# Router products from the merged activations' place, in high and low parts, and another order of the last scatters

## The chip, the cores and the metric

The kernel runs on one core of one Trainium2 chip. The metric is the device time of one execution in microseconds. TensorE (PE) multiplies, VectorE (DVE) and ScalarE (ACT) work element by element, GpSimd (POOL) also issues indirect DMAs, and SyncE (SP) issues the direct ones.

## The reference

One layer of a decoder over 2048 tokens of 1024 channels: two parallel branches (a recurrence and latent attention), a gated merge and an output projection, and then a mixture of 32 experts with two experts for each token. The part that the change touches is the router and what it feeds:

```python
x = x + merged @ w_out                       # output projection, residual
h = rmsnorm(x, ffn_norm_g)
p_group = softmax(h @ w_group + b_group)     # 4 groups
fine    = h @ w_router + b_router            # 32 experts; the best group's 8 are kept
top_v, top_i = top_k(fine_sel, 2)
gate = softmax(top_v) * gate_g
# the rows of each expert are gathered, go through SwiGLU, are weighted by gate and added to x
```

## The kernel before, in words

The program has stages: projections, recurrence and attention (to about 1750 us), `phase_f` (merges, output projection, router; to about 2160 us), the experts (to about 2660 us) and a final norm. Large products are made in fp32r from high and low parts: `mm3` issues three matmuls (lines 151 to 153) for each product, and `split` makes the parts, the high one by a copy on ACT (line 143) and the low one by a subtraction on DVE or POOL (line 144).

`phase_f` goes over four quarters of 512 tokens. In a quarter, `merge` makes eight pieces (`d`) of the merged activations: 24 matmuls each into PSUM "fm", two multiplications by the gate `gt` (line 1220), an addition (line 1221) and the split into the tiles `m`, high and low, which have one buffer each. The weights w_b come for each piece by SP into one raw buffer `wbr`, and are split into `wb`. Then, for each of the quarter's four tiles of 128 tokens, `project` makes two halves of 24 matmuls ("fo") and adds x into `xr`, and `router` transposes the tile by eight transposes (line 1240), copies the transposes on ACT into the fp32 tile `h2T` (line 1242, one buffer), and multiplies by the 36 router columns (line 1245, PSUM "fr"): 8 products, 16 records of 128x36 in the profile. A normalised tile `h` (line 1253) is stored to `h2d` for the experts' gathers.

`route` then finds the two experts on DVE (short instructions from line 1327 on, ending in `r_both`), counts the places by two small matmuls on PE (lines 1358 and 1359: `trib`, `onesb`), and computes the slots `si` on DVE (line 1371). Two indirect DMAs on POOL scatter the token's number to the lists `tokl` (one of each pair takes `r_t`, made at line 1373 with two buffers). After each quarter, `gates` makes the weights and scatters them to `wl` by eight more indirect DMAs. All scatters into one list wait for the one before them in that list.

At the end SP loads the lists as `ix`, POOL gathers rows of `h2d` into `xg`, and PE transposes them (line 1540) and starts on the experts. The lists of weights are read as `wx`, behind which SP's queue holds the weights of the expert after next. A list scheduler sets the order of instructions on each engine; engines take them in that order, so an instruction that waits holds all behind it on its engine.

## Time and profile before

| | |
|---|---|
| median of 3 runs | 2710.06 us (2707.57 to 2715.52) |
| the profiled execution | 2706.18 us |
| its span, first to last instruction | 2704.4 us |
| mean granted TensorE clock | 0.963 |
| busy: PE, DVE, ACT, POOL | 92%, 72%, 53%, 36% |

Shares are means over the whole span; the stages differ. The span is 1.8 us shorter than the execution's time, and the profiled execution is 3.9 us below the median.

### The profile page before, as it was taken

The numbers are of one execution on the slowest core, as the hardware profiler recorded it, in microseconds if no ns is written. First come the engines' busy times: TensorE is split into PE (matmuls) and PEld (weight loads), VectorE is DVE, ScalarE is ACT, GpSimd is POOL, SyncE is SP. The second block draws the span as 40 slices with busy tenths as digits, with TensorE's granted clock in tenths as the row PEclk, the third lists the DMA queues.
The fourth block names the chain that finished last, engine by engine and source line by source line (L and its number), as shares of the span: only waits on it lengthen the run. The fifth ranks groups of instructions, "written<-read, shape, count | busy, mean of one in ns | idle before, by whom it ended". The sixth has DMA issues, their size and how long they took to land. (4 is left out here: it accounts for less than half of the span.)

```text
span 2704.4 us, 42459 instructions
## 1 busy us (share of the span) xinstructions
PE 2493.0 (92%) x14868; PEld 2033.2 (75%) x14868; DVE 1957.0 (72%) x3466; ACT 1424.3 (53%) x2539; POOL 961.8 (36%) x676
## 2 busy tenths in 40 slices
PE   8999999999999998989999999999999878999991
PEld 6777778788787886767777777777888667989880
DVE  8766699777748994676666766666666678888883
ACT  6554243465443423666776767632232246878774
POOL 3111612401112222556665665402012145555540
PEclk9999999999999998999999999999999979999995
DMA  4556444435563435444443441674554377999987
GB/s 147 125 146 172 137 140 134 171 102 133 142 177 105 138 122 173 129 122 133 129 123 95 129 129 41 205 225 137 184 167 148 125 228 235 329 288 318 299 246 264
DMA packets 334443, 452.46 MB, mean 167 GB/s; under 512 B 170320, under 2 KB 216272, under 8 KB 332944
## 3 DMA queue, kind: packets, MB, share of 16 engines
q1 hardware_dynamic: 320656, 416.03, 49.3%
q0 software_dynamic: 13568, 33.67, 5.5%
q8 instruction: 118, 1.93, 0.3%
q14 instruction: 101, 0.83, 0.1%
HBM read 318.06 MB, written 138.33 MB: 169 GB/s over the span
## 5 line engine op out<-in xcount | busy, mean ns | idle before, releaser
L151 PE MATMUL am<-h,aw 128*128 128x512 f32 x1104 | 440.8, 400 | 21.2 <-ACT h L237 8.5
L144 POOL TENSOR_TENSOR pl<-pf,ph 128x512 fp32r<-128x512 f32 (+1 forms) x320 | 372.8, 1181 | 238.5 <-ACT ph L143 163.3
L153 PE MATMUL am<-h,aw 128*128 128x512 f32 x1104 | 437.8, 397 | 11.9 <-POOL aw L144 7.5
L152 PE MATMUL am<-h,aw 128*128 128x512 f32 x1104 | 437.3, 396 | 0.1
L1562 PE MATMUL gg<-hh,gu 128*128 128x256 f32 (+5 forms) x1024 | 271.0, 338 | 5.4 <-DVE hh L144 5.0
L151 PEld LDWEIGHTS am<-h,aw 128*128 128x128 f32 x1104 | 210.8, 191 | 70.1 <-ACT h L237 8.5
L153 PEld LDWEIGHTS am<-h,aw 128*128 128x128 f32 x1104 | 210.3, 191 | 60.3 <-POOL aw L144 8.7
L1563 PE MATMUL gg<-hh,gu 128*128 128x128 f32 (+5 forms) x1024 | 249.2, 250 | 0.0
L152 PEld LDWEIGHTS am<-h,aw 128*128 128x128 f32 x1104 | 210.5, 191 | 48.6 <-DVE h L238 2.4
L1052 ACT ACTIVATE pf<-st 128x512 f32<-128x512 f32 (+1 forms) x320 | 167.6, 529 | 119.2 <-PE st L1046 65.2
L1562 PEld LDWEIGHTS gg<-hh,gu 128*128 128x128 f32 x1024 | 195.8, 191 | 13.1 <-DVE hh L144 6.6
L1563 PEld LDWEIGHTS gg<-hh,gu 128*128 128x128 f32 x1024 | 198.6, 194 | 4.5
L143 ACT ACTIVATE ph<-pf 128x512 fp32r<-128x512 f32 (+1 forms) x320 | 176.8, 565 | 6.6
L985 DVE TENSOR_REDUCE mx<-sh 128x1 f32<-128x512 f32 x192 | 128.2, 686 | 66.1 <-PE sh L982 64.9
L144 POOL TENSOR_TENSOR aw<-awr,aw 128x1024 fp32r<-128x1024 f32 (+1 forms) x32 | 89.0, 2782 | 241.2 <-ACT aw L143 231.0
L144 DVE TENSOR_TENSOR gu<-graw,gu 128x1024 fp32r<-128x1024 f32 x128 | 155.0, 1239 | 12.0 <-ACT gu L143 10.3
L143 ACT ACTIVATE gu<-graw 128x1024 fp32r<-128x1024 f32 x128 | 131.1, 1056 | 33.8 <-DMA graw<-in_moe_w_gu 31.4
L801 DVE TENSOR_TENSOR inv<-inv,invt 128x62 f32<-128x62 f32 (+30 forms) x124 | 137.9, 1112 | 2.8
L144 POOL TENSOR_TENSOR sum<-sq,sum 128x512 fp32r<-128x512 f32 x16 | 23.5, 1469 | 317.1 <-ACT sum L143 301.3
L799 DVE TENSOR_TENSOR invt<-inv 128x62 f32<-128x62 f32 (+30 forms) x124 | 133.5, 1076 | 2.6
L1044 PE MATMUL st<-aq,ak 97*128 97x512 f32 (+1 forms) x320 | 127.5, 398 | 8.0 <-ACT pf L1052 7.1
L1580 POOL DMA_INDIRECT x2d<-yo,ix x50 | 93.0, 1860 | 104.2 <-DMA x2d<-yo,ix 21.5
(414 smaller groups left out, 6342.8 us busy)
## 6 DMA issues: line engine op xcount, KB each, us to landing
graw<-in_moe_w_gu SPq DMA_DIRECT2D x128, 512.0 KB
awr<-in_w_cols SPq DMA_DIRECT2D x70, 512.0 KB
draw<-in_moe_w_down SPq DMA_DIRECT2D x62, 512.0 KB
gate<-gsb SPq DMA_DIRECT2D x64, 256.0 KB
SC<-SCd SPq DMA_DIRECT2D x32, 512.0 KB
wbr<-in_w_b SPq DMA_DIRECT2D x32, 512.0 KB
gt<-gate SPq DMA_DIRECT2D x32, 512.0 KB
xs<-in_xT SPq DMA_DIRECT2D x32, 256.0 KB
```

Of the source, the lines that this page charges most:

```text
L143: nc.scalar.activation(hi, src, AF.Copy)
L144: (eng or nc.vector).tensor_tensor(out=lo, in0=src, in1=hi.bitcast(F32), op=OP.subtract)
L151: nc.tensor.matmul(ps, lh, rh, start=first and i == 0, stop=False)
L152: nc.tensor.matmul(ps, lh, rl, start=False, stop=False)
L153: nc.tensor.matmul(ps, ll, rh, start=False, stop=last and i == n - 1)
L799: V.tensor_tensor(out=tv, in0=m[:, 0:t, t:t + 1].to_broadcast([128, t, n]), in1=m[:, t:t + 1, t + 1:].to_broadcast([128, t, n]), op=OP.mult)
L801: V.tensor_tensor(out=m[:, 0:t, t + 1:], in0=m[:, 0:t, t + 1:], in1=tv, op=OP.add)
L985: V.reduce_max(mx[:, j, kb:kb + 1], ps[:, :n], axis=AX)
L1044: T.matmul(ps[:, cs], kk[0][:, ks], qq[0][:, cs], start=True, stop=False)
L1052: A.activation(pf[:, cs], ps[:, cs], AF.Exp, scale=SCALE)
L1562: T.matmul(*a, start=k == 0, stop=False)
L1563: T.matmul(*b, start=False, stop=k == 7)
```

## The change

The router's own fp32 tile `h2T` goes. The transposes are split, high on ACT and low on DVE, into the columns of `m` that belong to the same tile, whose merged activations have been read by then. The router's weights are split once into `wr2` (36 high and 36 low columns). For each of 8 channel blocks there is one product of the high part with all 72 columns and one of the low part with the 36 high ones, both in fp32r. ACT copies the 36 low sums out of PSUM (`lglo`) and DVE adds them. For the last tile, `h` and its store are written behind its routing, and the last quarter's gates are issued behind the last scatter to `tokl`.

```diff
--- before.py
+++ after.py
@@ -1203,6 +1203,9 @@
             wr = p.tile([128, 8, 36], F32, name="wr")
             self.dma(wr, I["w_r"])
             V.tensor_tensor(out=wr, in0=wr, in1=self.pv[:, 55:63, None].to_broadcast([128, 8, 36]), op=OP.mult)
+
+            wr2 = p.tile([128, 8, 72], F32R, name="wr2")
+            self.split(wr2[:, :, :36], wr2[:, :, 36:], wr)
             br = p.tile([128, 36], F32, name="br")
             self.dma(br, bcast(I["b_r"], 36))
 
@@ -1230,29 +1233,41 @@
                               for k in range(8)])
                 V.scalar_tensor_tensor(xt[:, ns], ps, 0.5, xt[:, ns], op0=OP.mult, op1=OP.add)
 
-            def router(i, xt):
+            def router(i, xt, m):
                 st_ = p.tile([128, 4], F32, name="fstat", bufs=2)
                 h = p.tile([128, D], F32, name="h2")
-                hT = p.tile([128, 8, 128], F32, name="h2T")
+
+                hT = [t[:, :, i % 4 * 128:(i % 4 + 1) * 128] for t in m]
                 for b in range(2):
                     ps = self.pst("fo", 3)
                     for k in range(4):
                         T.transpose(ps[:, k * 128:(k + 1) * 128], xt[:, (4 * b + k) * 128:(4 * b + k + 1) * 128],
                                     self.ident)
-                    A.activation(hT[:, 4 * b:4 * b + 4], ps.rearrange("p (k t) -> p k t", k=4), AF.Copy)
+                    self.split(hT[0][:, 4 * b:4 * b + 4], hT[1][:, 4 * b:4 * b + 4], ps.rearrange("p (k t) -> p k t", k=4))
                 ps = self.pst("fr", 2)
                 for k in range(8):
-                    T.matmul(ps[:, :36], hT[:, k], wr[:, k], start=k == 0, stop=k == 7)
+                    T.matmul(ps[:, :72], hT[0][:, k], wr2[:, k], start=k == 0, stop=False)
+                    T.matmul(ps[:, :36], hT[1][:, k], wr2[:, k, :36], start=False, stop=k == 7)
+                lo = p.tile([128, 36], F32, name="lglo", bufs=2)
+                A.activation(lo, ps[:, 36:72], AF.Copy)
                 A.activation(h, xt, AF.Square, accum_out=st_[:, 0:1])
                 A.activation(st_[:, 1:2], st_[:, 0:1], AF.Sqrt, scale=1.0 / D, bias=self.eps[:, 0:1])
                 V.reciprocal(st_[:, 2:3], st_[:, 1:2])
                 yield
                 lg = p.tile([128, 36], F32, name="lg", bufs=2)
-                V.scalar_tensor_tensor(lg, ps[:, :36], st_[:, 2:3], br, op0=OP.mult, op1=OP.add)
+                V.tensor_tensor(out=lo, in0=ps[:, :36], in1=lo, op=OP.add)
+                V.scalar_tensor_tensor(lg, lo, st_[:, 2:3], br, op0=OP.mult, op1=OP.add)
                 self.dma(self.x2d[i * 128:(i + 1) * 128, :], xt)
-                V.scalar_tensor_tensor(h, xt, st_[:, 2:3], g_bc, op0=OP.mult, op1=OP.mult)
-                self.dma(self.h2d[i * 128:(i + 1) * 128, :], h)
+
+                def rows():
+                    V.scalar_tensor_tensor(h, xt, st_[:, 2:3], g_bc, op0=OP.mult, op1=OP.mult)
+                    self.dma(self.h2d[i * 128:(i + 1) * 128, :], h)
+
+                if i < NT - 1:
+                    rows()
                 yield from self.route(p, i, lg)
+                if i == NT - 1:
+                    rows()
                 if i % 4 == 3 and i < NT - 1:
                     self.gates(self.cp, i // 4)
 
@@ -1287,13 +1302,14 @@
                     if last:
                         step(last, 2)
                     project(i, m, xt, 1)
-                    g = router(i, xt)
+                    g = router(i, xt, m)
                     if i == NT - 1:
                         step(g, 1)
                     if last:
                         step(last, 1)
                     last = g
             step(last, 2)
+            self.placed = self.last_place
 
     def gates(self, p, q):
 
@@ -1313,7 +1329,7 @@
                 self.scatter(self.wl[j], self.si[:, j, i:i + 1], self.gate_w[:, j, i:i + 1])
 
     def scatter(self, dst, idx, src):
-        self.nc.gpsimd.indirect_dma_start(out=dst, out_offset=bass.IndirectOffsetOnAxis(ap=idx, axis=0),
+        return self.nc.gpsimd.indirect_dma_start(out=dst, out_offset=bass.IndirectOffsetOnAxis(ap=idx, axis=0),
                                           in_=src, in_offset=None, bounds_check=NE * CAP - 1, oob_is_err=False)
 
     def route(self, p, i, lg):
@@ -1372,7 +1388,7 @@
         t1 = t("t1", 1, I32)
         V.tensor_scalar(t1, self.c["tok"][:, i:i + 1], float(-S), None, op0=OP.add)
         for j, src in enumerate((self.toki[:, i:i + 1], t1)):
-            self.scatter(self.tokl[j], self.si[:, j, i:i + 1], src)
+            self.last_place = self.scatter(self.tokl[j], self.si[:, j, i:i + 1], src)
 
     def route_end(self, p):
 
@@ -1610,7 +1626,8 @@
             xg = {0: x_load(0), 1: x_load(1)}
             V.tensor_copy(ixf, ix)
             self.ranks(p, ixf, ix)
-            self.gates(self.cp, 3)
+            with tc.issue_after(self.placed.ins):
+                self.gates(self.cp, 3)
             for j in range(2):
                 self.dma(wxr[j][:, 0:2], lists(self.wl, j))
```

The rows below show how the engines' orders differ at three places. On PE at the boundary between the first and the second quarter, before: the counting product of tile 2 stands inside the second merge (`wb_18989`), with tile 3's router behind it.

```order
L153 MATMUL fm<-y_18381,wb_18990 128x512
L151 MATMUL fm<-y_18381,wb_18989 128x512 [waits DVE_49]
L1358 LDWEIGHTS trib
L1358 MATMUL fr<-r_both,trib 128x32 [waits DVE_49]
L1359 LDWEIGHTS onesb
L1359 MATMUL fr<-run,onesb 128x32
L1245 MATMUL fr<-wr,h2T 128x36 x4
L1245 MATMUL fr<-wr,h2T 128x36 [waits Activation_49]
L1245 MATMUL fr<-wr,h2T 128x36 x3
L152 MATMUL fm<-y_18382,wb_18989 128x512
```

After: they stand one and a half merges further on, behind the third merge's first half (`wb_19135`), and the second quarter's projection follows at once, reading the new `m_18920` (high) and `m_18921` (low). The router reads the old ones, `m_18034` and `m_18035`; both generations are the same place in memory.

```order
L153 MATMUL fm<-y_18384,wb_19135 128x512
L1374 LDWEIGHTS trib [waits DVE_49]
L1374 MATMUL fr<-r_both,trib 128x32 [waits PE_49]
L1375 LDWEIGHTS onesb
L1375 MATMUL fr<-run,onesb 128x32
L1249 MATMUL fr<-wr_18023,m_18034 128x72
L1250 MATMUL fr<-wr_18023,m_18035 128x36
...
L1250 MATMUL fr<-wr_18023,m_18035 128x36
L151 MATMUL fo<-wo_18016,m_18920 128x512 [waits Activation_49]
...
L153 MATMUL fo<-wo_18016,m_18921 128x512 [waits DVE_49]
```

What moved: the counting product and the last router of a quarter now stand later, and the new `m` is written only when that router has read the old one. On DVE at the same boundary, before: `r_both` of tile 2 stands ahead of the third merge's weights (`wb_19084`).

```order
L1351 TENSOR_TENSOR oh_16823<-r_o_18801,r_o_18823 128x32 [waits DVE_49]
L1220 SCALAR_TENSOR_TENSOR gt<-gt,fm 128x512 [waits PE_49]
L1248 RECIPROCAL fstat<-fstat 128x1 [waits Activation_49]
L1355 TENSOR_TENSOR r_both<-oh_16822,oh_16823 128x32 [waits DVE_49]
L144 TENSOR_TENSOR m_18882<-gt,m_18881 128x512 [waits Activation_49]
L1253 SCALAR_TENSOR_TENSOR h_18923<-xr,fstat,g_bc 128x1024 [waits DMAHW3_49,DVE_49]
...
L144 TENSOR_TENSOR wb_19084<-wbr,wb_19083 128x1024 [waits DMAHW6_49,Activation_49]
...
L1360 TENSOR_TENSOR run<-run,r_both 128x32 [waits PE_49]
```

After, where the weights of the second, third and fourth merge are `wb_19041`, `wb_19135` and `wb_19174` (low parts):

```order
L1367 TENSOR_TENSOR oh_16823<-r_o_18840,r_o_18862 128x32 [waits DVE_49]
L144 TENSOR_TENSOR wb_19174<-wbr,wb_19173 128x1024 [waits DMAHW1_49,PE_49,Activation_49]
L1371 TENSOR_TENSOR r_both<-oh_16822,oh_16823 128x32 [waits DVE_49]
L1376 TENSOR_TENSOR run<-run,r_both 128x32 [waits DVE_49,PE_49]
L1379 SCALAR_TENSOR_TENSOR r_rb<-fr,cst 128x32
...
L1387 TENSOR_TENSOR si<-r_over,r_slot 128x2 [waits DVE_49]
L144 TENSOR_TENSOR m_18921<-gt,m_18920 128x512 [waits PE_49,Activation_49]
```

What moved: `r_both` of tile 2 now stands behind `wb_19174`, the low part of the fourth merge's weights. On POOL at the end of the stage, before (tiles 14 and 15, weights of the last quarter, then the gathers):

```order
L1316 DMA tokl_16810<-toki,si 8192x1 [waits DMASW4_49,DVE_49]
L1316 DMA tokl_16811<-r_t_21714,si 8192x1 [waits DMASW5_49]
L1316 DMA wl_16812<-gate_w,si 8192x1 [waits DMASW0_49,DVE_49]
L1316 DMA wl_16813<-gate_w,si 8192x1 [waits DMASW1_49,DVE_49]
L1316 DMA tokl_16810<-toki,si 8192x1 [waits DMASW6_49,DVE_49]
L1316 DMA tokl_16811<-r_t_21775,si 8192x1 [waits DMASW7_49]
L1316 DMA wl_16812<-gate_w,si 8192x1 [waits DMASW0_49]
L1316 DMA wl_16813<-gate_w,si 8192x1 [waits DMASW1_49]
L1316 DMA wl_16812<-gate_w,si 8192x1 [waits DMASW4_49]
L1316 DMA wl_16813<-gate_w,si 8192x1 [waits DMASW5_49]
L1501 DMA xg_21800<-h2d,ix 128x1024 [waits DMAHW4_49,DMAHW5_49,DMAHW2_49,DMAHW6_49,DMAHW0_49,DMAHW7_49,DVE_49,PE_49]
L1501 DMA xg_21801<-h2d,ix 64x1024 [waits PE_49,Pool_49]
```

After:

```order
L1332 DMA tokl_16810<-toki,si 8192x1 [waits DMASW4_49,DVE_49]
L1332 DMA tokl_16811<-r_t_21908,si 8192x1 [waits DMASW5_49]
L1332 DMA tokl_16810<-toki,si 8192x1 [waits DMASW6_49,DMASW0_49,DVE_49]
L1332 DMA tokl_16811<-r_t_21968,si 8192x1 [waits DMASW7_49,DMASW1_49]
L1332 DMA wl_16812<-gate_w,si 8192x1
L1332 DMA wl_16813<-gate_w,si 8192x1
L1332 DMA wl_16812<-gate_w,si 8192x1 [waits DMASW2_49]
L1332 DMA wl_16813<-gate_w,si 8192x1 [waits DMASW3_49]
L1517 DMA xg_21995<-h2d,ix 128x1024 [waits DMAHW4_49,DMAHW2_49,DMAHW5_49,DMAHW1_49,DMAHW6_49,DMAHW0_49,DMAHW7_49,DVE_49,PE_49]
...
L1332 DMA wl_16812<-gate_w,si 8192x1 [waits DMASW4_49]
L1332 DMA wl_16813<-gate_w,si 8192x1 [waits DMASW5_49]
L144 TENSOR_TENSOR dn_22095<-draw,dn_22094 128x1024 [waits DMAHW4_49,PE_49,Activation_49]
```

What moved: the four scatters to `tokl` stand together, four scatters to `wl` follow them rather than six with two among the `tokl` ones, and the last of `wl` stand behind the gathers and the split of an expert's weights. On DVE the last tile's `h` keeps its place ahead of the last tile's logits in both orders.

## Rows read from the trace of the kernel before

**Rows 1.** TensorE's groups of instructions between 1750 and 2160 us, the stage of merges, output projection and router, with different shapes apart: count, busy us, mean ns, and what ended the idle time before them.

```profile
L152 PE MATMUL fo<-wo,m 128*128 128x512 f32 x255 | 101.7, 400 | 0.0
L1245 PE MATMUL fr<-wr,h2T 128*128 128x36 f32 x256 | 31.7, 275 | 1.6 <-ACT h2T L1242 1.6
```

**Rows 2.** Busy time of each engine in stretches of the same stage (length, then PE, PEld, DVE, ACT, POOL busy, granted clock, DMA share); the first lies within a quarter, the second holds a boundary between two.

```profile
1895.00:1940.00 45.00, 45.00 (x223) 37.16 (x222) 26.50 (x80) 13.56 (x20) 1.94 (x2) 1.00 0.62 200
1940.00:1990.00 50.00, 50.00 (x246) 41.05 (x245) 35.39 (x126) 14.08 (x20) 14.58 (x14) 1.00 0.48 159
```

**Rows 3.** What TensorE waited for between 1750 and 2190 us: us in total, times, longest.

```profile
PE gt L1540 <- DMA xg<-h2d,ix: 18.3, 1, 18.3
PE fr L1358 <- DVE r_both L1355: 5.5, 2, 5.0
PE fm L151 <- DVE gt L1220: 5.0, 2, 4.6
```

**Rows 4.** TensorE's weight loads in the same stage by form: busy us, mean ns.

```profile
L151 PEld LDWEIGHTS fo<-wo,m 128*128 128x128 f32 x253 | 47.7, 189 | 11.4 <-ACT m L143 1.0
L1245 PEld LDWEIGHTS fr<-wr,h2T 128*128 128x128 f32 x256 | 31.1, 191 | 2.7 <-ACT h2T L1242 1.9
L1358 PEld LDWEIGHTS <-trib 128*128 128x128 bf16 x16 | 1.6, 101 | 3.8 <-issue 3.8
```

**Rows 5.** TensorE in time (start, us): first a pair of fp32r products with 256 and 128 columns in the stage of experts, then the end of the projections and the start of the experts.

```profile
2330.43 0.34 PE L1562 MATMUL gg<-hh,gu 128*128 128x256 f32 x1
2330.66 0.33 PE L1562 MATMUL gg<-hh,gu 128*128 128x256 f32 x1
...
2144.70 0.97 PE L1245 MATMUL fr<-wr,h2T 128*128 128x36 f32 x8
2145.51 0.48 PE L151 MATMUL fo<-wo,m 128*128 128x512 f32 x1
...
2148.61 0.40 PE L153 MATMUL fo<-wo,m 128*128 128x512 f32 x1
2148.84 0.98 PE L1245 MATMUL fr<-wr,h2T 128*128 128x36 f32 x8
...
2176.46 1.97 PE L1540 MATMUL gt<-cst,xg 128*128 128x128 f32 x8 [18.30 <-DMA xg<-h2d,ix]
```

**Rows 6.** ACT in time: half of a tile's transposes copied for the router, and the high part of w_b for the fourth merge (d=3) behind the first quarter boundary.

```profile
1851.28 0.60 ACT L1242 ACTIVATE h2T<-fo 128x512 f32<-128x512 f32 x1 [0.28 <-PE fo L1240]
1861.22 1.06 ACT L143 ACTIVATE wb<-wbr 128x1024 fp32r<-128x1024 f32 x1 [5.54 <-DMA wbr<-in_w_b]
```

**Rows 7.** DVE in time over the same boundary: a subtraction for the merged activations, the one for the fourth merge's w_b, and the stop at r_t (the bracket says how long DVE stood and on what).

```profile
1851.10 0.69 DVE L144 TENSOR_TENSOR m<-gt,m 128x512 fp32r<-128x512 f32 x1
1862.32 1.22 DVE L144 TENSOR_TENSOR wb<-wbr,wb 128x1024 fp32r<-128x1024 f32 x1 [0.69 <-issue]
...
1890.78 0.15 DVE L1373 TENSOR_SCALAR r_t<-cst 128x1 int32<-128x1 f32 x1 [5.79 <-DMA tokl<-r_t,si]
```

**Rows 8.** SyncE's queue in time over the same boundary: the load of w_b for the fourth merge.

```profile
1856.45 0.33 SPq L96 DMA_DIRECT2D wbr<-in_w_b  x1
```

**Rows 9.** TensorE in time over the same boundary: the counting product of tile 2, a small stop behind a split of w_b, and the stop behind DVE.

```profile
1854.09 0.19 PE L1358 MATMUL fr<-r_both,trib 128*128 128x32 bf16 x1
...
1877.17 0.50 PE L151 MATMUL fm<-y,wb 128*128 128x512 f32 x1 [0.56 <-ACT wb L143]
...
1892.18 0.80 PE L151 MATMUL fm<-y,wb 128*128 128x512 f32 x1 [4.58 <-DVE gt L1220]
```

**Rows 10.** GpSimd in time over the same boundary: the scatters of the first quarter's weights, and tile 3's places behind them.

```profile
1878.41 1.48 POOL L1316 DMA_INDIRECT wl<-gate_w,si  x1 [3.99 <-DMA wl<-gate_w,si]
1883.40 0.97 POOL L1316 DMA_INDIRECT wl<-gate_w,si  x1 [2.22 <-DMA wl<-gate_w,si]
1886.13 0.97 POOL L1316 DMA_INDIRECT tokl<-r_t,si  x1 [0.30 <-issue]
```

**Rows 11.** DVE in time at the end of the stage: h of tile 15, its logits and its slots.

```profile
2151.81 1.28 DVE L1253 SCALAR_TENSOR_TENSOR h<-xr,fstat,g_bc 128x1024 f32<-128x1024 f32 x1
2153.12 0.25 DVE L1251 SCALAR_TENSOR_TENSOR lg<-fr,fstat,br 128x36 f32<-128x36 f32 x1
...
2159.07 0.22 DVE L1371 TENSOR_TENSOR si<-r_over,r_slot 128x2 int32<-128x2 f32 x1
```

**Rows 12.** GpSimd in time at the end of the stage: the last tile's first scatter to `tokl`, scatters to `wl`, and the first gather.

```profile
2160.38 0.97 POOL L1316 DMA_INDIRECT tokl<-toki,si  x1 [0.31 <-issue]
2162.93 0.97 POOL L1316 DMA_INDIRECT wl<-gate_w,si  x1 [0.31 <-issue]
2164.21 0.97 POOL L1316 DMA_INDIRECT wl<-gate_w,si  x1 [0.30 <-issue]
2165.49 0.97 POOL L1316 DMA_INDIRECT wl<-gate_w,si  x1 [0.31 <-issue]
2169.00 0.97 POOL L1316 DMA_INDIRECT wl<-gate_w,si  x1 [2.54 <-DMA graw<-in_moe_w_gu]
2170.28 1.53 POOL L1501 DMA_INDIRECT xg<-h2d,ix  x1 [0.30 <-issue]
```

**Rows 13.** SyncE's queue at the load of the weights' lists, and ACT's first use of the expert weights wx.

```profile
2180.79 5.01 SPq L96 DMA_DIRECT2D wx<-wl  x8
...
2208.12 1.27 ACT L1589 ACTIVATE yo<-gd,wx 128x512 f32<-128x512 f32 x2
```

## Prediction

> **What bounds the kernel now.** I read the stages first. In the stage of merges and router TensorE is the engine that sets the pace: in a stretch within a quarter it is busy for all of 45.00 us, and in one that holds a quarter boundary for all of 50.00 us, at a granted clock of 1.00, while DVE is busy for 26.50 and 35.39 us [rows 2]. So work added to DVE or ACT there is free until TensorE waits for it, and time of TensorE counts one for one. Then I read what TensorE does wait for: 5.0 us for the gate's product on DVE, nearly all in one stop of 4.58 us at 1892.18, and at the end 5.5 us for `r_both` and 18.3 us for the first gather [rows 3, 9]. Two chains matter, therefore: that of the quarter boundaries, and that of the end, where TensorE stands for 18.30 us until 2176.46 [rows 5].
>
> The stop at 1892.18 is a head-of-line stop. DVE stood 5.79 us at `r_t` until 1890.78, because that needs an earlier scatter to `tokl` to have landed [rows 7]. This one left POOL at 1886.13 only, behind scatters to `wl` before which POOL had stood for 3.99 and 2.22 us, since each waits for its predecessor's landing [rows 10].
>
> **The products.** A tile's router had 16 matmul records, 256 for 16 tiles [rows 1]. Eight of them take 0.81 us from the first to the next instruction (2144.70 to 2145.51), so 0.101 us each and 1.62 us a tile [rows 5]. After, there are 16 fp32r matmuls with 72 and 36 columns, each with a load of 128 columns. Their price is not in the trace; the nearest row is a pair of fp32r products with 256 and 128 columns, 0.23 us for the pair, so at most 0.115 us each and 1.84 us a tile [rows 5]. The load of an fp32r weight takes 189 ns, and of the router's fp32 weight 191 ns [rows 4], so I take no change on TensorE, with bounds of -1 and +3.5 us (16 times 0.22) over the stage.
>
> The trace's bf16 load takes 101 ns, about half of the others [rows 4]. The Trainium skill (TensorE: Matmul & The Clock Gate, "Weight-path perf modes") says that fast weight load is on for 128 weights whose type is not FP32, and that FP32 gains nothing. Read so that fp32r is no FP32, the rule would halve the router's loads; the fp32r row of 189 ns says that it doesn't. By the rule the sum below would be smaller by some 12 us; by the row nothing changes.
>
> **The splits.** The two ACT copies of a tile, 0.60 us each [rows 6], stay, with another destination. New on DVE are two subtractions of 0.69 us (the row of a 128x512 one [rows 7]) and an addition of about 0.2, on ACT a copy of 36 columns of about 0.2: some 1.6 us of DVE a tile, 25 us in all. They lie under TensorE: a quarter has 4 x 1.6 = 6 us more DVE work, against 14 to 18 us idle in each stretch of rows 2. Without that cover they would cost all of it. One split of 128x288 for `wr2` lies at the stage's beginning and is taken at nothing.
>
> **The boundaries.** With the order of after, tile 2's counting product stands behind 11 + 12 = 23 more merge matmuls than before. They take 0.23 us each (2148.61 to 2148.84, a matmul of 512 columns as theirs [rows 5]), so TensorE comes there at 1854.09 [rows 9] + 5.4 = 1859.5. But `r_both` of tile 2 now stands on DVE behind the fourth merge's low weights. These weights are loaded at 1856.45 [rows 8], split on ACT at 1861.22 [rows 6] and subtracted on DVE from 1862.32 to 1863.54 [rows 7]; this chain has one raw buffer and isn't shortened. So `r_both` is ready at about 1863.7, and TensorE waits 4.2 us. Behind it the old `m` is read by tile 3's router, and only then may ACT write the new `m`, which the next projection reads at once: a copy of 0.60 us and the signals on both sides, 0.9 us. Against these 5.1 us stand the 4.58 us of the old stop and 0.56 us behind a split of w_b [rows 9], the same 5.1. The old stop's cause, `tokl` behind `wl` on POOL, is still there; with one and a half merges of shift I leave 1.5 us of it (between 0 and 4.6). The first boundary is thus 5.1 + 1.5 - 5.1 = +1.5 us. At the second and the third boundary TensorE had no or nearly no wait. The new wait on `m` comes there too, and `r_both` stands ahead of its neighbour's low weights rather than behind, so that the stop is milder: I take +2 and +1.5 us, between 0 and 5.1 each. All together +5.0 us, bounds -4 (first boundary -5.1, little at the others) and +14.
>
> **The end.** Tile 14's router (1.62 us) and tile 13's counting now stand behind the last projection, which thus begins at 2148.61 - 1.7 = 2146.9 [rows 5]. From there I walk: x is added by 2148.2; TensorE does tile 14's router and then tile 15's second transposes until 2149.4; ACT has the square of the tile (1.2 us) and the high copy (0.60) until about 2151.1; DVE has `h` of the last tile (1.28 us, still ahead [rows 11]) and then the low subtraction until 2152.4; the second half of tile 15's router ends at 2153.3, and its logits are there at 2153.9, against 2153.12 before [rows 11]. From these logits to the slots DVE took 5.95 us for 40 instructions (2153.12 to 2159.07), 0.149 us each; after there are 54, since tile 14's routing is now interleaved: 8.0 us. So the slots come at 2161.9, 2.8 us late. POOL then gives 1.0 back, for the first scatter of tile 15 left 1.31 us behind the slots [rows 11, 12], being queued behind `wl`, and now leaves some 0.3 behind them: `tokl` and `ix` are 1.8 us late. In front of the gather stand four scatters to `wl`, and the fourth waits for the landing of the second. What such a landing takes differs: at most 2.56 us for the scatter of 2162.93 (its successor left at 2165.49), 4.79 us for that of 2164.21 (2169.00), beside which expert weights were loaded [rows 12]. The loads stand beside them in after as well, so I take 4.8: the gather leaves about 1.5 us later than 2170.28, bounds -3 (the walk on DVE too pessimistic) and +5.
>
> The Trainium skill (DMA: Bandwidth & Descriptors, "Anatomy of one DMA") puts a GpSimd DMA at about 2.0 us plus its bytes' time. By that the fourth scatter would wait for nothing and the gather leave at about the old time, so that the sum would be smaller by 1.5 us. The row with 4.79 us disagrees.
>
> Behind the gathers, the last pair of scatters to `wl` now stands behind the split of an expert's weights, so `wx` is loaded some 6 us after 2180.79, and the weights behind it on SP too. ACT first needs `wx` at 2208.12 [rows 13], which leaves more than 10 us behind the permutation; 0 us, at most +2.
>
> **Sum.** 0 + 0 + 5.0 + 1.5 = +6.5 us on the profiled execution's 2706.18, so 2712.7; that execution is 3.9 us below the runs' median, so 2716.6 as a median. What a measurement can tell from no change is 0.3%, 8 us: 2702 to 2718.
>
> **Rivals.** *Faster:* the head-of-line stop goes (-5.1 at the first boundary), the others are hidden since DVE runs ahead of TensorE, and the end gains: slots no later, and 1.1 us less queueing and a shorter row of `wl`, -3. Then 2710 - 8.1 = 2702, at the edge of what can be told. For it speaks that POOL's order at the end is better; against it that `r_both` stands behind a DMA chain with one buffer. It decides at the point where DVE has `r_both` ready by 1859.5. *Slower:* the same wait at every boundary, 3 x 5.1, the old stop not gone, and the end at +3: 2710 + 18 = 2728. It needs `r_both` to wait for w_b at all three boundaries. *No effect:* the waits cancel and the median stays at 2710; that holds if the interleaved routing at the end costs what POOL gives. *Fast loads* for fp32r, by the rule above: a router matmul at 0.101 x 101/191 = 0.053 us, 0.77 us a tile less, 12 us over all; with the +6.5 of the other terms 2704.5.
>
> **Chances.** My sum 0.40, no effect 0.17, slower 0.25, faster 0.15, fast loads 0.03. My sum's own spread (2710 to 2723) puts about a third of it above 2718, and a tenth of the slower case stays below it. Faster by over 0.3% is 0.18 (the case, and tails of the others), slower 0.36, within 0.46. The range is 2699 to 2731: from just beyond the faster case to just beyond the slower one.
>
> **What the profile will show.** Right: TensorE with a wait for `r_both` of 3 to 5 us once near 1860 and smaller ones near 1965 and 2060, waits for the split of `m` just behind them; the router's 16 records in 1.6 to 1.8 us; tile 15's slots near 2162 plus what the boundaries added; the fourth `wl` scatter behind an idle time. Wrong: no wait at the counting products, or the router's products at another pace than a load each; or a wait for `wx` or weights in the first experts, which I count as hidden.

## The result

The changed kernel takes 2729.94 us (median of 17 runs, 2717.44 to 2738.44); before takes 2707.57 us (17 runs, 2701.22 to 2715.52). By all runs together the ratio is 1.0076, with a 95% interval of 1.0064 to 1.0089: slower by about 21 us. The profiled execution has a span of 2729.5 us at a granted clock of 0.957.

To see in which stage the time went, I take the first and the last start of four groups: the merges on TensorE, the projections, the transposes of gathered rows, and ACT's weighting of the experts' outputs. These are the rows of the changed kernel (durations in ns are minimum, median and maximum; then the first and the last start):

```profile
L151 PE MATMUL fm<-y,wb x256: 387/389/628, 1735.8 to 2119.7; 128*128 128x512 f32 x128
L153 PE MATMUL fo<-wo,m x256: 387/395/796, 1754.1 to 2166.1; 128*128 128x512 f32 x128
L1556 PE MATMUL gt<-cst,xg x400: 270/272/476, 2197.2 to 2638.6; 128*128 128x128 f32 x134
L1605 ACT ACTIVATE yo<-gd,wx x64: 665/682/720, 2235.9 to 2671.3; 128x512 f32<-128x512 f32 x64
```

From the first merge to the last projection are 430.3 us, from there to the first gathered rows 31.1, and on to the last weighting 474.1. The same in all profiled executions but that of e10 (below):

| kernel | ahead of the merges | merges to last projection | to the gathered rows | experts | TensorE's waits in the second stage | clock lost there |
|---|---|---|---|---|---|---|
| before | 1732.0 | 416.6 | 27.9 | 468.9 | 7.1 | 1.6 |
| before, again (e12) | 1732.4 | 419.6 | 28.2 | 475.2 | 9.0 | 3.5 |
| changed | 1735.8 | 430.3 | 31.1 | 474.1 | 13.4 | 8.8 |
| changed, again (e11) | 1730.1 | 431.4 | 31.6 | 474.6 | 17.9 | 5.1 |
| e1 router alone | 1738.9 | 431.0 | 34.1 | 475.1 | 18.0 | 5.1 |
| e2 scatters alone | 1736.2 | 420.4 | 27.5 | 484.8 | 11.1 | 3.5 |
| e3 own half tiles | 1734.7 | 430.2 | 36.4 | 481.3 | 15.3 | 10.4 |
| e4 8 tiles r_t | 1721.9 | 419.6 | 27.8 | 471.1 | 7.4 | 3.6 |
| e5 r_both first | 1736.0 | 442.7 | 33.6 | 464.1 | 22.5 | 15.3 |
| e6 own last tile | 1727.6 | 427.5 | 33.8 | 476.5 | 15.8 | 6.8 |
| e7 16 tiles r_t | 1736.2 | 411.7 | 28.3 | 466.0 | 1.5 | 1.7 |
| e8 e5 with 16 | 1730.2 | 436.7 | 33.7 | 464.3 | 16.0 | 10.6 |
| e9 e2 with 16 | 1741.6 | 407.4 | 27.1 | 488.6 | 1.8 | 1.8 |

All in us. The waits are those that the profile lists for TensorE from 80 us behind the first merge to the last projection; a wait of 2.7 to 3.8 us for `y`, which every one of these executions has at 72 to 75 us, lies ahead of that. "Clock lost" sums 1 minus the granted clock over stretches of 5 us in the same part, so it counts some of the idle time too. The first column is the same program in all kernels and spreads over 20 us in single executions, so a single time says little here, and a stage is compared with its like.

Most of the loss is in view: the second stage has 11.9 us more than in four executions with before's order there (mean 430.9 of the changed kernel, its repeat and e1, against 419.0 of before, its repeat, e2 and e4), the way to the gathered rows 3.4 us more. These make 15 of the 21 us; the experts and what is left to chance come below. TensorE's waits in the changed kernel, in us, times and longest, which answer to [rows 3]:

```profile
PE gt L1556 <- DMA xg<-h2d,ix: 17.6, 1, 17.6
PE fr L1374 <- DVE r_both L1371: 8.3, 4, 3.0
PE fm L151 <- ACT y L143: 7.1, 4, 3.5
PE fm L151 <- DVE gt L1223: 3.3, 2, 1.9
PE fo L151 <- ACT m L143: 2.7, 4, 1.2
```

In before, the view of [rows 3] has this line for `y`:

```profile
PE fm L151 <- ACT y L143: 3.3, 1, 3.3
```

The reader sees that the gate's product has gone from 5.0 to 3.3 us, but the counting products wait in four places rather than two, and waits for the split of `m` (2.7 us) and more for `y` (7.1 us against 3.3) have come. The first boundary in time, on TensorE:

```profile
1865.65 0.19 PE L1374 MATMUL fr<-r_both,trib 128*128 128x32 bf16 x1 [1.54 <-DVE r_both L1371]
1865.71 0.28 PE L1249 MATMUL fr<-wr,m 128*128 128x72 f32 x1
1865.82 0.26 PE L1250 MATMUL fr<-wr,m 128*128 128x36 f32 x1
...
1867.42 0.41 PE L1249 MATMUL fr<-wr,m 128*128 128x72 f32 x1
1867.63 0.38 PE L1250 MATMUL fr<-wr,m 128*128 128x36 f32 x1
...
1868.97 0.80 PE L151 MATMUL fo<-wo,m 128*128 128x512 f32 x1 [0.53 <-ACT m L143]
```

The counting product waits 1.54 us, the router follows, and in its midst the distance of two products grows from 0.11 to 0.21 us. The stretches there (length, busy PE, PEld, DVE, ACT, POOL, granted clock, DMA share, GB/s) show the reason:

```profile
1862.00:1867.00 5.00, 3.46 (x23) 2.77 (x21) 3.10 (x17) 1.06 (x1) 0.00 (x0) 0.97 0.17 43
1867.00:1870.00 3.00, 2.47 (x10) 2.16 (x11) 1.40 (x6) 1.24 (x3) 1.94 (x2) 0.50 0.37 144
1870.00:1873.00 3.00, 3.00 (x9) 2.32 (x8) 1.83 (x10) 0.00 (x0) 0.00 (x0) 0.50 0.64 90
1873.00:1876.00 3.00, 3.00 (x13) 2.17 (x12) 1.33 (x5) 0.00 (x0) 0.00 (x0) 0.92 0.67 260
```

The clock is at 0.50, the lower of its two levels (1.2 GHz), until about 1873. This happens four times in the profiled execution from the first boundary on (near 1866, 1925, 1980 and 2085), in before once, behind the stop of [rows 9]. By the measure of the table the four cost 3.4, 1.7, 1.7 and 1.7 us.

### The profile page after: what moved, and what is told of

Same layout as the page of the kernel before. It is cut to its first block, busy times and chain, and to the rows that moved or that the text cites. A ratio compares the mean times of both kernels' runs of the same rounds, so it can differ in the third digit from the quotient of the medians.

```text
span 2729.5 us, 42521 instructions
## 1 busy us (share of the span) xinstructions
PE 2508.2 (92%) x14868; PEld 2042.9 (75%) x14868; DVE 1978.1 (72%) x3515; ACT 1426.9 (52%) x2556; POOL 966.1 (35%) x676
## 4 chain that ended last, share of the span: by engine, by line
PE 31%; issue 10%; DVE 7%; DMA 7%; ACT 4%; POOL 1%; SPq 0%; POOLq 0%; DVEq 0%; ACTq 0%
PE gg L1578 3%; PE st L1044 2%; PE sh L982 2%; PE pv L1036 2%; PE pv L1031 2%; PE st L1045 2%; PE st L1046 2%; PE pv L1032 2%; DMA graw<-in_moe_w_gu 2%; DVE gu L144 2%; PE gg L1579 1%; ACT dn L143 1%; DMA zx<-x2d 1%; PE gt L1556 1%; DMA tokl<-r_t,si 1%
## 5 line engine op out<-in xcount | busy, mean ns | idle before, releaser
L1578 PEld LDWEIGHTS gg<-hh,gu 128*128 128x128 f32 x1024 | 197.5, 193 | 13.6 <-DVE hh L144 4.9
L985 DVE TENSOR_REDUCE mx<-sh 128x1 f32<-128x512 f32 x192 | 128.3, 686 | 65.3 <-PE sh L982 64.1
```

The source lines that it names most:

```text
L985: V.reduce_max(mx[:, j, kb:kb + 1], ps[:, :n], axis=AX)
L1578: T.matmul(*a, start=k == 0, stop=False)
```

## The experiments

**Each half alone.** e1 is the changed kernel without these two edits, e2 is before with them:

```diff
-                if i < NT - 1:
-                    rows()
+                rows()
                 yield from self.route(p, i, lg)
-                if i == NT - 1:
-                    rows()
...
-            with tc.issue_after(self.placed.ins):
-                self.gates(self.cp, 3)
+            self.gates(self.cp, 3)
```

> The changed kernel with the order of the last scatters and of the last tile's rows as before: the router's part of the change alone. Theory (the router's later place makes the boundary waits, and TensorE's clock falls behind them): the stage of merges loses its 16 us here too, and the time is 1.006 to 1.008 of before; the granted clock falls at the three boundaries. Rival (the scatters' order costs it, through the later lists of weights): within 0.2% of before.

> The kernel before with the order of the last scatters and of the last tile's rows as changed: the other part alone. Theory: the last tile's first place is scattered about 1 us earlier, the fourth scatter of weights waits for a landing as before, and the first gather leaves between 1.5 us earlier and at the same time; the lists of weights come 5 to 7 us later and are hidden; time within 0.1% of before. Rival: the later lists hold back the experts, and the stage of experts is 4 to 5 us longer (1.0015 or more).

The edit to `rows()` doesn't show in the traces: the last tile's `h` starts ahead of that tile's logits with it (the changed kernel at 2169.30 and 2173.97) as without it (e1 at 2173.05 and 2177.72). What e1 and e2 tell apart is the gates' place. Measured: e1 1.0095 (1.0074 to 1.0116), e2 1.0057 (1.0037 to 1.0076). Neither theory held whole: each half costs, and the two together (1.0152) twice what the whole change does. By the table the two are different things. e1 repeats the longer merges (431.0) and lengthens the way to the gathered rows to 34.1 us; in e2 that way is 27.5, against 27.9, 28.2 and 27.8, as was expected, but the experts take 484.8 us. In e1 POOL shows what the scatters' new place is worth once the routing is late:

```profile
2184.55 0.97 POOL L1329 DMA_INDIRECT wl<-gate_w,si  x1 [0.30 <-DVE wx L1530]
2187.10 0.97 POOL L1329 DMA_INDIRECT tokl<-toki,si  x1 [0.30 <-issue]
2196.02 0.97 POOL L1329 DMA_INDIRECT wl<-gate_w,si  x1 [2.85 <-DMA wl<-gate_w,si]
2197.29 1.37 POOL L1514 DMA_INDIRECT xg<-h2d,ix  x1 [0.30 <-issue]
```

The last tile's first place leaves at 2187.10, behind two scatters to `wl` (2184.55 and the next), and the first gather at 2197.29, behind a fourth scatter that stood 2.85 us. With the scatters' new order this way is 31.1 and 31.6 us, without it 34.1, 33.6, 33.8 and 33.7 (e1, e5, e6, e8): 2.5 us won, where the router is changed, and about 0.5 where it is not (e2).

**The experts' order.** The scheduler writes another order of the expert stage for e2: compared row by row, half of TensorE's order there differs from before, while the changed kernel's differs in about one per cent. What TensorE waited for in e2's expert stage, and in the same stage of before:

```profile
PE gd L151 <- ACT at L1579: 11.3, 8, 5.5
PE gd L153 <- DVE at L1582: 7.2, 9, 1.6
```

```profile
PE gd L151 <- ACT at L1571: 4.5, 8, 1.3
PE gd L153 <- DVE at L1574: 4.0, 5, 1.4
```

The second products (`gd`) wait for the activations (`at`) for 18.5 us rather than 8.5. e9 repeats e2's expert order in a program with another merge stage:

> The kernel of e2 (order of the last scatters alone) with the sixteen tiles for r_t of e7; its order of the experts on TensorE is e2's, and half of it differs from the kernel before. Theory (the experts' order that the scheduler writes out behind the scatters' new place costs the 14 us that e2's stage of experts was longer): that stage takes 480 us or more again, the stage of merges 411 to 414 as in e7, and the time is 1.002 to 1.003 of before. Rival (one disturbed execution): 466 to 472 us for the experts and 0.996 to 0.998.

Measured: 1.0014 (1.0000 to 1.0029), a little less than expected, with 407.4 us for the merges (expected 411 to 414) and 488.6 for the experts. The theory on the experts holds: two executions with that order took 484.8 and 488.6 us, nine with before's own (before, e4, e7, e12) or one within about a per cent of it (the changed kernel, e11, e5, e6, e8) 464 to 477. So e2's loss goes with this order and not with the later lists: in the changed kernel the lists are read as late (at 2207.04, 9.9 us behind the start of TensorE's transposes, 10.0 in e2, against 4.3 in before [rows 5, 13]) and its experts take 474. e3's order, 7% from e2's, took 481.3 us. Another order is not always longer: e1's, a third one, differs from before's by nearly half, too, and took 475.1. What in e2's order costs the time stays open, since in e9 the same waits for `at` make 14.8 us, and those for `hh` 18.8 rather than 12.1 in before and 12.5 in e2.

**The tiles of its own.** In e3 each half of a tile has its own place and the products follow it at once; in e6 only the last tile of a quarter has such a place, while the products follow each half in all tiles:

```diff
+                    if i % 4 == 3:
+                        hT = [p.tile([128, 4, 128], F32R, name="h2T%d" % j) for j in range(2)]
+                    else:
+                        hT = [t[:, 4 * b:4 * b + 4, i % 4 * 128:(i % 4 + 1) * 128] for t in m]
```

> The changed kernel, but the high and low parts of the router's input lie in two tiles of their own of half the size (one buffer each, used twice a tile) and not in the merged activations' place. Theory (the new merged activations' wait for the last router and its later place make the stalls, and the stalls the fall of the clock): the waits for the split of m behind a router go, the clock falls at most once, as before, and about 3 us (16 times 0.17 of the products' pace) stay, 1.001 to 1.003 of before. Rival (the narrow fp32r products themselves let the clock fall): the clock falls at each boundary, or oftener, with no wait of over 1 us there, and the time stays at 1.006 or more.

> The router's part of the change alone (last scatters as before), but the last tile of each quarter has its high and low parts in two half-size tiles of their own, so that the new merged activations wait for no router. The order of the experts is that of the kernel before within half a per cent. Theory: the waits of the projections for the split of m at the boundaries go, r_both's stay; the stage takes 424 to 428 us, the time is 1.004 to 1.006 of before. Rival (the wait for the old m decides): the stage takes 420 to 423 us, 1.002 to 1.003.

Measured: e3 1.0093 (1.0072 to 1.0114), e6 1.0058 (1.0036 to 1.0080). In e3 the waits for `m` went, as the theory had it, and those for `r_both` too, but the time went against its number. It does not decide, for other stops came on TensorE in their place,

```profile
1936.64 1.11 PE L1245 MATMUL fo<-cst,xr 128*128 128x128 f32 x4 [5.64 <-DVE xr L1234]
...
2128.40 0.40 PE L1250 MATMUL fr<-wr,h2T 128*128 128x36 f32 x1 [3.30 <-DVE h2T L144]
```

and the clock's falls lie behind these and one of 1.78 us. The second is one of the half tiles' own; the first isn't: `xr` stood on DVE behind `r_t`:

```profile
1935.83 0.15 DVE L1390 TENSOR_SCALAR r_t<-cst 128x1 int32<-128x1 f32 x1 [8.95 <-DMA tokl<-r_t,si]
```

In e6 the waits for `m` did not go. The merge stage took 427.5 us, in the range of the first theory, but for other reasons, one of them to be seen on DVE:

```profile
1908.54 0.15 DVE L1393 TENSOR_SCALAR r_t<-cst 128x1 int32<-128x1 f32 x1 [7.28 <-DMA tokl<-r_t,si]
```

DVE stood 7.28 us at `r_t`, the head-of-line stop of [rows 7], and the low part of `m` for which TensorE waited 5.42 us until 1910.48 stood behind it. Another wait, of 4.16 us until 1900.46, ended ahead of that stop: there the high part of `m` stood on ACT behind a split of w_b, for whose load ACT had stood 9.33 us.

**r_both ahead of the weights.** e5 is e1 with the splits of the third and fourth w_b issued behind `r_both`:

```diff
-        self.split(hl[0], hl[1], raw)
+        with (self.tc.issue_after(after.ins) if after is not None else ExitStack()):
+            self.split(hl[0], hl[1], raw)
```

> The router's part of the change alone (order of the last scatters as before), and the splits of w_b for the third and fourth merge of a quarter are issued behind r_both of the quarter before's third tile. The order of the experts on TensorE is within half a per cent of that of the kernel before, which it was not in the first run of the router's part alone (e1). Theory (stops at the counting product, and the clock's falls behind them, are the larger part of the stage's loss): the waits of 1 to 2 us for r_both at the boundaries go, the clock falls there at most once, the stage of merges takes 421 to 425 us from its first merge to its last projection (417 to 420 before, 430 to 431 with the change), and the time is 1.003 to 1.005 of before. Rival (the boundary's work is late anyway, and w_b now waits for r_both): the stop moves to the next merge, the stage takes 429 us or more, 1.006 or more.

Measured: 1.0108 (1.0083 to 1.0133), with 442.7 us for the merges. The rival held, and worse: the scheduler put the counting products earlier on TensorE, where they wait 5.39, 2.31 and 2.66 us; TensorE waits 8.11 us for the gate's product, too, and DVE's longest stop at `r_t` grew to 9.3 us:

```profile
DVE r_t L1389 <- DMA tokl<-r_t,si: 17.4, 3, 9.3
```

**r_t without reuse.** e4 gives `r_t` eight tiles, e7 sixteen:

```diff
-        t1 = t("t1", 1, I32)
+        t1 = p.tile([128, 1], I32, name="r_t1", bufs=16)
```

> The kernel before with eight buffers rather than two for r_t (its tile is named apart), so that DVE doesn't stop there for the scatter to land. Theory: the stop of 4.58 us of TensorE near 1892 and the fall of its clock behind it (about 1.7 us) go: 5 to 6 us faster, 0.998. Rival: the stop only moves to the next instruction on DVE that needs the scatters, no change.

> The kernel before with sixteen tiles for r_t, one for each tile of tokens, all made at the stage's beginning, so that DVE never waits there for a scatter to land (with eight the ninth was issued at the same early place and waited for the first). The order of the experts is unchanged. Theory: the stop of 3.5 to 4.9 us at the first boundary and the clock's fall behind it go, 0.998 of before. Rival: another wait ends as late, and nothing changes.

e4 measured 1.0000 (0.9986 to 1.0014). All eight were written at the start, those from the ninth on were issued as early as a tile came free, and DVE stopped there as before (3.20 us at 1826.27, 4.76 at 1880.98). e7 measured 0.9969 (0.9955 to 0.9983), faster than before and than the changed kernel. Its merges took 411.7 us, and of TensorE's waits from the first boundary to the experts three groups of [rows 3] and of its neighbours now read:

```profile
PE fr L1358 <- DVE r_both L1355: 5.5, 2, 5.0
PE fr L1245 <- ACT h2T L1242: 1.5, 2, 1.3
PE fm L151 <- DVE gt L1220: 0.2, 1, 0.2
```

The stop cost at least its own 4.6 us: 416.6 and 419.6 us became 411.7, and e2's 420.4 became 407.4 in e9. The clock stays up at that boundary.

> The kernel of e5 with sixteen tiles for r_t. Theory: DVE's stops at r_t held the merges of the second quarter too; 2 to 5 us less than e5, so 1.001 to 1.004 of before. Rival: these stops lay beside TensorE's work there: the same as e5 within 1 us.

e8 measured 1.0051 (1.0032 to 1.0069), 436.7 us for the merges, 6.0 less than e5: DVE's stops held the merges there too, by a little more than expected. By the ratios e8 is some 15 us faster than e5, and the stages show no more than these 6: between the two profiled executions another 5.8 us lie ahead of the merges, where the programs don't differ. Two stretches of e8 also show the clock behind two waits of like length:

```profile
1967.95 0.21 PE L1374 MATMUL fr<-r_both,trib 128*128 128x32 bf16 x1 [2.30 <-DVE r_both L1369]
...
2133.26 0.50 PE L151 MATMUL fo<-wo,m 128*128 128x512 f32 x1 [2.40 <-DVE xr L1235]
```

```profile
1966.00:1971.00 5.00, 3.05 (x16) 3.06 (x17) 4.12 (x25) 0.00 (x0) 0.30 (x1) 0.67 0.18 48
1971.00:1976.00 5.00, 5.00 (x17) 4.09 (x18) 3.57 (x10) 2.29 (x4) 1.65 (x2) 0.65 0.55 119
2131.00:2136.00 5.00, 2.75 (x12) 2.24 (x13) 3.17 (x6) 3.32 (x5) 1.58 (x1) 1.00 0.28 111
2136.00:2141.00 5.00, 5.00 (x32) 4.34 (x31) 0.69 (x1) 1.01 (x2) 0.83 (x1) 1.00 0.52 168
```

At 1967.95 a wait of 2.30 us is followed by the router's products; the clock falls (0.67 and 0.65). At 2133.26 a wait of 2.40 us lies between projections; the clock stays at 1.00. This is no rule. All twelve waits for `r_both` at the boundaries of the changed kernel, e11, e1, e5 and e8 (1.13 to 5.39 us) have a fall behind them. But a wait amid the last quarter's router, which the kernels without the router's change have, was followed by a fall in e4, e7 and e9 and by none in before, e12 and e2:

```profile
2112.94 1.08 PE L1245 MATMUL fr<-wr,h2T 128*128 128x36 f32 x8 [1.33 <-ACT h2T L1242]
```

```profile
2110.69 1.08 PE L1245 MATMUL fr<-wr,h2T 128*128 128x36 f32 x8 [1.26 <-ACT h2T L1242]
```

The first is before's, the second e7's, where the clock from 2111 to 2116 is 0.66.

**The change with r_t mended.**

> The changed kernel with sixteen tiles for r_t. Theory: DVE's stops at r_t hold the merges behind the boundaries here too (waits for the gate's product of 1.4 to 1.9 us and falls of the clock), and go: the stage of merges takes 421 to 427 us instead of 430. Its order of the experts is a third one, which may take anything between 466 and 485 us; the time is 1.003 to 1.009. Rival: the stage of merges is as long as before this, 429 to 431, since r_both and the wait for m decide.

Measured: 1.0072 (1.0043 to 1.0102), as the changed kernel itself. The time lies in the theory's range, but its only profiled execution took 8427.15 us and is not read, so theory and rival, which differ in the stage of merges, are not told apart, and where the 16 tiles' gain went is open; this program's order of the experts is near e1's.

> The changed kernel a second time, for a second profiled execution: what of its stages' lengths repeats. If the program's order sets them: 428 to 432 us for the merges, 31 from the last projection to the first gathered rows, 472 to 476 for the experts. If chance does: the experts between 464 and 472.

> The kernel before a second time, for a second profiled execution. If the order sets the lengths: 416 to 421 us for the merges, 28 to the first gathered rows, 466 to 471 for the experts; what comes ahead of the merges lies between 1722 and 1739 by chance.

The merges (431.4 and 419.6) and the way to the gathered rows (31.6 and 28.2) repeat within 3 us. The experts of before took 475.2 us the second time, above the 466 to 471 expected: there chance is as large as the 4 us by which the changed kernel's mean lies above the mean of before, e4, e7 and e12, and whether these 4 us are the change's stays open.

## Why the prediction was right and wrong

It forecast slower, by 6.5 us, with 2716.6 the likeliest and 2731 the upper end. The measured 2729.94 lies just inside. The direction and the end were right; of the boundaries' term the waits that the prediction named came out near their size, and what it put at nothing, other waits and the clock, made up most of the difference.

**The end** was right. From the start of the last projection the walk had the last tile's logits 7.0 us on, its slots at 15.0, the first gather at 24.9. On TensorE, DVE and POOL:

```profile
2166.12 0.48 PE L153 MATMUL fo<-wo,m 128*128 128x512 f32 x1
```

```profile
2173.97 0.25 DVE L1259 SCALAR_TENSOR_TENSOR lg<-lglo,fstat,br 128x36 f32<-128x36 f32 x1
2180.52 0.16 DVE L1387 TENSOR_TENSOR si<-r_over,r_slot 128x2 int32<-128x2 f32 x1
```

```profile
2181.16 0.97 POOL L1332 DMA_INDIRECT tokl<-toki,si  x1 [0.67 <-DVE wx L1533]
2183.71 0.97 POOL L1332 DMA_INDIRECT wl<-gate_w,si  x1 [0.30 <-issue]
2184.99 0.97 POOL L1332 DMA_INDIRECT wl<-gate_w,si  x1 [0.31 <-issue]
2186.26 0.97 POOL L1332 DMA_INDIRECT wl<-gate_w,si  x1 [0.30 <-issue]
2189.66 0.97 POOL L1332 DMA_INDIRECT wl<-gate_w,si  x1 [2.43 <-DMA wl<-gate_w,si]
2190.94 1.53 POOL L1517 DMA_INDIRECT xg<-h2d,ix  x1 [0.31 <-issue]
```

The logits came 7.85 us behind 2166.12, the slots at 14.4, the gather at 24.8. That the sum fits to 0.1 us is in part luck: the logits were 0.85 us later than in the walk, and the way from them to the slots took 6.55 us rather than 8.0. The first place leaves 0.64 us behind its slots, and the fourth scatter to `wl` waits 2.43 us for a landing. It leaves, at 2189.66, 4.7 us behind the second scatter's 2184.99, as in [rows 12] (4.79), while SyncE's queue holds loads of expert weights from 2185.04 on. The Trainium skill (DMA: Bandwidth & Descriptors, "Anatomy of one DMA") puts such a DMA at about 2.0 us and its bytes' time. The trace does not agree for this scatter, which had only 128 rows of one number to move; the scatter before it, 2.55 us ahead of its own successor, leaves room for the 2.0 us. The term was +1.5, and 3.4 less the 1.7 us of work moved behind the projection is +1.7.

**The products** were priced at nothing, with an upper bound of 3.5 us. In the trace two starts lie 0.111 us apart (1865.71 and 1865.82), 1.78 us a tile against 1.62: +2.5 us over sixteen tiles. No change was taken where the row of 0.115 us for an fp32r product [rows 5] was the nearer. The forms of the products and of their loads read:

```profile
L1249 PE MATMUL fr<-wr,m 128*128 128x72 f32 x128 | 30.7, 285 | 0.0
```

```profile
L1249 PEld LDWEIGHTS fr<-wr,m 128*128 128x128 f32 x128 | 25.4, 198 | 0.6 <-DVE lglo L1258 0.3
```

No fast load shows: such a load takes 198 ns, where the fp32 one took 191 [rows 4], and the products' starts are not at the 0.053 us of that rival. The Trainium skill (TensorE: Matmul & The Clock Gate, "Weight-path perf modes") has fast weight load on for 128 weights whose type is not FP32. Read so that fp32r is no FP32, it does not agree with this trace.

**The boundaries** were the term that was too small: +5.0 forecast, with +14 the upper bound. Worked out from the table, the stage has 11.9 + 1.7 = 13.6 us more work and waiting than before, of which 2.5 are the products: 11 us. The waits grew by 7.8 us (16.4 as a mean of the changed kernel, e11 and e1 against 8.7 of before, e12, e2 and e4), and the clock lost 3.2 us more (6.3 against 3.1 in the same executions; part of it is idle time that the waits hold too). So 2.5, 7.8 and 3.2 make 13.5.

By what TensorE waited for, as means of the same executions in us:

| wait | before | changed | difference | forecast |
|---|---|---|---|---|
| `r_both` and the new `m` | 0 | 7.7 | +7.7 | +8.6 |
| the gate's product, the router's copy, w_b | 8.7 | 4.4 | -4.3 | -3.6 |
| `y` and `xr` | 0 | 4.3 | +4.3 | 0 |
| the clock | 3.1 | 6.3 | +3.2 | 0 |

The forecast's 8.6 is 5.1 at the first boundary, 2 and 1.5 at the others; its -3.6 is what it took off the old stops. So the waits that the prediction named, new and old, came out near their sum, and the steps that failed are two terms that it left at nothing. The first is the waits for `y` and `xr`. The longest of them on DVE and then TensorE:

```profile
1921.45 1.23 DVE L1188 TENSOR_TENSOR yin<-yin 128x1024 f32<-128x1024 f32 x1 [5.84 <-DMA yin<-Rcd]
```

```profile
1923.82 0.50 PE L151 MATMUL fm<-y,wb 128*128 128x512 f32 x1 [2.46 <-ACT y L143]
```

DVE stood 5.84 us for loaded rows just ahead of it, so the splits on DVE, which the prediction counted as hidden, were not what ended this wait. SyncE issued those loads at 1914.31 only; what made them late, the splits, the new order or the stops at `r_t` (28.7 us of DVE in the changed kernel, 25.1 in before), no run here tells apart. The second is the clock: it was left out, and falls at all three boundaries and behind `y`, in before only behind the old stop.

Within the first line the parts differ from the forecast. The wait behind `r_both` at the first boundary was put at 4.2 us and measured 1.54: DVE reads

```profile
1863.38 0.15 DVE L1389 TENSOR_SCALAR r_t<-cst 128x1 int32<-128x1 f32 x1 [1.58 <-DMA tokl<-r_t,si]
1864.28 1.23 DVE L144 TENSOR_TENSOR wb<-wbr,wb 128x1024 fp32r<-128x1024 f32 x1
1865.42 0.17 DVE L1371 TENSOR_TENSOR r_both<-oh,oh 128x32 bf16<-128x32 bf16 x1
```

so the fourth merge's low weights did stand ahead of `r_both`. The changed kernel's first merge starts 3.8 us later than before's, so times are counted from there. The low weights ended at 1865.51, 129.7 us on, 1.8 earlier than the 131.5 of the walk (1863.54); TensorE came at 1864.11, 128.3 us on, 0.8 later than its 127.5 (1859.5). The chain of [rows 6, 7, 8] thus ended a little earlier, where the prediction took it as fixed. The waits for the new `m`, put at 0.9 us each, measured 0.53, 0.62 and 1.17 at the three boundaries, but 2.4 to 2.5 more stands in e11 (at 1901.30) and e1 (at 1909.17) behind the first one. `r_both` made TensorE wait 1.17 us at the second boundary and not at all at the third. Of the signs that the prediction named, the one wait of 3 to 5 us near 1860 failed so; the waits behind it for `m`, the router's pace of a load for each product and the idle time ahead of the fourth scatter came.

Of the rivals, "slower" came nearest (2728), but not for its reason: it named the same wait of 5.1 us at every boundary, and the loss was made of smaller waits, waits elsewhere, falls of the clock and the products. Boundaries, products and end together make 9 of the some 14 us by which the forecast fell short; 4 more may lie in the experts, as said above, and the rest is within the spread of single executions.

## What to carry to other kernels

Where an engine takes its instructions in order, price a moved wait by what stands beside it: here each stop of 1 to 5 us for `r_both`, ahead of narrow products, came with a fall of the clock, 1.7 us or more, while several of 2 us among wide products cost their length alone. Neither is a rule, so set a chance of a fall into the sum. And follow the waits beyond the place that the edit moves: the largest term that was missed, 4.3 us, stood for other tiles. A tile with two buffers that is handed to a DMA can hide a wait for all that stands ahead of it on that queue; sixteen tiny tiles were worth 0.3% here, eight nothing. And if a list scheduler orders a program, compare its order in stages that the edit doesn't touch before an experiment is read: half of an edit (e2) can cost time in a stage that it doesn't touch, because that stage was written out anew.

## What the runs showed of the hardware

TensorE's granted clock stayed at its upper level over a wait of 2.40 us between projections and fell to the lower over one of 1.17 or 2.30 us that the router's products followed (the changed kernel at 1976.49, e8 at 1967.95). But a wait of 1.33 us amid the router's products left it up in before (2112.94), and one of 1.26 us at the same place let it fall in e7 (2110.69). It fell, too, over 2.46 us between merges (the changed kernel at 1923.82), where e11's 2.30 us at the same place left it up. The successor of a scatter by GpSimd in its list could leave only 4.7 us after it beside loads of weights (the changed kernel at 2184.99), and 2.55 us after it just before (2183.71). The part of the program ahead of the merges, the same instructions in every kernel, took between 1721.9 and 1741.6 us in thirteen executions.
